# Block sums made in the up projections and kept in DRAM; 49 seven-product pairs instead of 32

## Chip, core and metric

The kernel runs on one core of a Trainium2 chip. The metric is the time of one execution on the device in microseconds (us). Before the change it is 2122.69 us, the median of three runs (2122.64 to 2122.83).

## The reference

A two-layer encoder trunk for 256 tokens of width 2048, all in float32. Each layer has an attention part (differential attention in layer 0, windowed grouped-query attention in layer 1, each beside four heads that look at 256 memory tokens, and one output projection) and a dense MLP. The change lies in the MLP:

```python
x = x + heads @ w_out[i]
h = rms_norm(x, norm_mlp[i])
x = x + jnp.square(jax.nn.relu(h @ w_up[i])) @ w_down[i]     # 2048 -> 8192 -> 2048
```

## The kernel before

**Three products for one.** TensorE multiplies a rounded float32 form. Each operand is split into a rounded part and a remainder by `split`: ScalarE casts (`hi`, L249), VectorE subtracts (`lo`, L250). A product is then hi x hi, hi x lo and lo x hi, added up in PSUM (`three`, L359 to L361). Weights come from DRAM in pieces of 128 x 1024 (512 KB), and every piece is split on arrival.

**Fetching.** `plan` lists all weight pieces in the order of use. `fetch` takes the next one, lets SyncE (SP) load it into a buffer `raw`, and splits it into `hi` and `lo`; there are four buffers of each. `piece` keeps two pieces ahead of the one in use. Other tiles come from three rings of 512 KB buffers: `x2` (8), `h2` (6), `blk` (10).

**The up projections** (L333 and L337) take 16 chunks of 512 columns. ScalarE and VectorE make the squared ReLU of each (L788 to L790) into a hidden tile of 512 KB; six of the sixteen lie in one large buffer (`big`, chunks 4 to 9), the other ten in `blk`. Chunk c holds hidden blocks j = 2c and 2c+1.

**The down projections** run in two halves of 1024 output columns, and in each through j = 0 to 31. A pair j is two weight pieces and one hidden block, which `h2_of` splits into a buffer of `h2`. An ordinary pair multiplies a 2 x 2 of blocks by a 2 x 2 of blocks in eight products, 24 matmuls. For the j in `FAST` (5, 8, ... 26, eight per half) the same result comes from **seven products** (`seven`, 21 matmuls). They need sums of blocks on both sides: of the weights, a and b, made from the two raw pieces in `fetch_sums` (L202, L204, L205) and split in turn into four tiles; of the hidden block, four differences made by `differences` (L370, L372, L373) and split (L249, L250 `h<-t2k`). Both halves make the differences of a block anew. The four extra accumulators (`side`) are folded into the outputs by `shared` after the half's last seven-product pair. The out projections have three such pairs in each layer (`OUT_FAST`).

The two halves use tiles of the same name, but a and b lie in `x2` except in the second half of layer 0, where the next layer's inputs take part of `x2`; there they lie in `blk`, as the hidden tiles come free.

**What sets the order.** The program is written in the order above; small jobs are `Task`s, of which `tick` runs one that is due after every piece, and `flush` all that are left. From this the tile layer's scheduler makes each engine's list of instructions, which is fixed when the program is built: it moves an instruction ahead where its data is ready. An engine works its list in order. A tile waits until the last readers of its buffer are done. SP's list holds all weight loads; POOL's has little: some loads at the start, sums in the memory part, and two masks (L673, L675) on the bias table that comes back into `big` for layer 1 (L671).

Of the kernel before, what the change touches and what calls it, by code (L numbers as in the profile page):

```python
# [14 lines left out]
F32 = mybir.dt.float32  # L15
# [7 lines left out]
P = 128  # L23
# [10 lines left out]
WAIT = 2  # L34
AHEAD = 2
WARM = 16
FAST = (5, 8, 11, 14, 17, 20, 23, 26)
LAM_INIT = 0.8 - 0.6 * math.exp(-0.3 * 0)

G_ATTN, G_MEM, G_MLP = 0, 2 * KT, 4 * KT  # L40
# [8 lines left out]
def trunk(ctx: ExitStack, tc: tile.TileContext, xin, xtok, memin, pos, rel, gcol, rows,  # L49
# [12 lines left out]
    def nm(s):  # L62
        uid[0] += 1
        return f"{s}{uid[0]}"
# [4 lines left out]
    def quad(tag, shape=(P, 2, 2, 256), dt=F32R):  # L69
        return xp.tile(list(shape), dt, tag=tag, name=nm(tag), bufs={"x2": 8, "h2": 6, "blk": 10}[tag])  # L70
# [92 lines left out]
    def flush():  # L163
        while tasks:
            next(t for t in tasks if t.can()).step()
# [9 lines left out]
    def fast_pairs(name, h):  # L175

        if name.startswith("out"):
            return OUT_FAST[h]
        return FAST if name.startswith("down") else ()

    def plan_pairs(name, n):
        plan.extend((name, h, j) for h in range(2) for j in range(2 * n))
# [10 lines left out]
    newest = [None]  # L193
    sums = {}

    def fetch_sums(key, raw, hi, lo):

        first = newest[0]
        out_ = key[0].startswith("out")
        tag = "blk" if out_ or key[:2] == ("down0", 1) else "x2"  # L200
        a, b = quad(tag, (P, 2, 512), F32), quad(tag, (P, 2, 512), F32)
        nc.vector.tensor_tensor(a, first.rearrange("p (a n) -> p a n", a=2),  # L202
                                raw[:, 512:1024].unsqueeze(1).broadcast_to([P, 2, 512]), op=ALU.add)
        nc.vector.tensor_tensor(b[:, 0, :], a[:, 1, :], first[:, 0:512], op=ALU.add)  # L204
        nc.vector.tensor_tensor(b[:, 1, :], b[:, 0, :], raw[:, 0:512], op=ALU.add)  # L205
        split(hi[:, 0:512], lo[:, 0:512], raw[:, 0:512])
        ah, al, bh, bl = [quad("blk" if out_ else "x2", (P, 2, 512)) for _ in range(4)]
        split(ah, al, a)
        split(bh, bl, b)
        sums[key] = (ah, al, bh, bl)  # L210

    def fetch(parts=1, lead=None):

        name, c, j = plan.popleft()
        src = weights[name][c, j]
        raw = wp.tile([P, 1024], F32, tag="raw", name=nm("raw"))
        hi = wp.tile([P, 1024], F32R, tag="hi", name=nm("hi"))
        lo = wp.tile([P, 1024], F32R, tag="lo", name=nm("lo"))
        n = 1024 // parts
        seven = j % 2 == 1 and j // 2 in fast_pairs(name, c)  # L220
        for i in range(parts):
            s = slice(i * n, (i + 1) * n)
            if lead is not None:
                lead(i)
            behind[0] = nc.sync.dma_start(raw[:, s], src[:, s])
            if seven:
                fetch_sums((name, c, j), raw, hi, lo)
            else:
                split(hi[:, s], lo[:, s], raw[:, s])
        newest[0] = raw  # L230
        ready.append(((name, c, j), hi, lo))
# [545 lines left out]

    def mlp(layer, X2, last):
        hT = []
        wide = big([P, 6, 4, S])  # L780
        for c in range(16):
            ps = chunk_out(f"up{layer}", c, 8, lambda k: X2[k], "mm" if c % 2 == 0 else "aux", 2 if c == 0 else 1)
            if c == 0:
                mlp_stats()
            ht = wide[:, c - 4] if 4 <= c < 10 else blk([P, 4, S], F32)
            for o in range(4):
                t = t1k()
                nc.scalar.copy(t, ps[o][:, 256:512])  # L788
                nc.vector.tensor_tensor(t, ps[o][:, 0:256], t, op=ALU.add)
                nc.vector.scalar_tensor_tensor(ht[:, o, :], t, 0.0, t, op0=ALU.max, op1=ALU.mult)  # L790
            hT.append(ht)
        N2 = Halves()

        def hidden(j):
            return hT[j // 2].rearrange("p k s -> p (k s)")[:, (j % 2) * 512:(j % 2) * 512 + 512]

        def h2_of(j):
            t2 = quad("h2", (P, 2, 512))
            split(t2[:, 0, :], t2[:, 1, :], hidden(j))
            return lambda kk, t, part: t2[:, part, kk * S + t * P:kk * S + (t + 1) * P]  # L800


        for half_ in range(2):
            tag = "mm" if half_ == 0 else "aux"
            ps = [[bank(tag) for _ in range(2)] for _ in range(2)]
            chunks = (2 * half_, 2 * half_ + 1)
            fast = fast_pairs(f"down{layer}", half_)
# [12 lines left out]
            held = []  # L820
            for j in range(32):
                if j == fast[0]:
                    side = [bank("aux" if half_ == 0 else "mm") for _ in range(4)]
                two = [piece(f"down{layer}", half_, 2 * j + i) for i in range(2)]
                at = h2_of(j)
                if last and half_ == 1 and j >= 30:
                    held.append((j, two, at))
                    continue
                if j in fast:
                    t2 = quad("h2", (P, 2, 512))  # L830
                    differences(t2, hidden(j))
# [168 lines left out]
```

## Time and profile before

| | |
|---|---|
| median of 3 runs | 2122.69 us |
| profiled execution | 2122.36 us, its span 2120.6 us |
| TensorE clock granted | 1.000 |
| TensorE / VectorE / ScalarE busy | 2110.4 / 1547.2 / 1141.0 us |
| layer 0: up projections | about 425 to 783 us |
| layer 0: down projections | about 783 to 1119 us |
| layer 1: up projections | about 1424 to 1780 us |
| layer 1: down projections | about 1780 us to the end |

The span runs from the first to the last instruction; the execution's own time is 1.76 us longer. PE is TensorE's matmuls, PEld its weight loads (they overlap), DVE is VectorE, ACT ScalarE, POOL GpSimd. A matmul's length is counted to its modelled end, so that neighbours overlap; what one costs is the distance between starts. In timeline rows the first number is the start, the second the length; in brackets is the idle time before it and what ended it. In group rows the numbers are the busy time, the mean length in ns, and the idle time before.

### The profile page before, as it was taken

To read this page: it belongs to the slowest core of one execution; us is meant where nothing else is said; L and a number is where in the kernel's file an instruction comes from. 1 tells how busy PE (TensorE), PEld (TensorE's weight loads), DVE (VectorE), ACT (ScalarE), POOL (GpSimd) and SP (SyncE) were. 2 spreads that over 40 slices of the span, in tenths; PEclk is the share of its full clock that TensorE was granted. 3 is DMA by queue.
4 is the path that set the end of the run, shared out by engine and by line. 5 is a ranking of instruction groups with operands and counts; after the bars stand their busy time and mean duration, and the time that the engine had idled before them with its cause. 6 is when DMAs were issued, how large, how long until landed. Compare 5 with 4: busy or idle time off the path is not lost.

```text
span 2120.6 us, 29406 instructions
## 1 busy us (share of the span) xinstructions
PE 2110.4 (100%) x11002; PEld 1786.8 (84%) x11002; DVE 1547.2 (73%) x2341; ACT 1141.0 (54%) x1732; POOL 34.9 (2%) x61
## 2 busy tenths in 40 slices
PE   9999999999999999999999999999999999999999
PEld 7878878888888888888888888888888888888887
DVE  7667788865565558889986677885655656888896
ACT  6456675554444445656655566564444444665564
POOL 1200020000000000000000000000000000000000
PEclk9999999999999999999999999999999999999999
DMA  8864464566666666565756555455666666566654
GB/s 295 239 210 150 159 192 156 190 181 196 188 188 190 189 189 204 193 200 198 257 200 190 179 168 184 152 190 187 187 190 189 185 195 189 193 216 206 207 190 159
DMA packets 114960, 409.24 MB, mean 193 GB/s; under 512 B 13568, under 2 KB 14336, under 8 KB 114560
## 3 DMA queue, kind: packets, MB, share of 16 engines
q1 hardware_dynamic: 111840, 401.01, 59.2%
q0 software_dynamic: 1536, 4.20, 0.8%
q10 hardware_dynamic: 1440, 2.15, 0.3%
q8 instruction: 86, 1.41, 0.3%
q14 instruction: 58, 0.48, 0.1%
HBM read 401.93 MB, written 5.37 MB: 192 GB/s over the span
## 4 chain that ended last, share of the span: by engine, by line
PE 96%; DMA 1%; DVE 1%; ACT 1%; issue 0%; POOL 0%; DVEq 0%; ACTq 0%; POOLq 0%
PE mm L333 11%; PE aux L333 11%; PE mm L360 7%; PE mm L359 7%; PE mm L361 7%; PE aux L360 7%; PE aux L359 7%; PE aux L361 7%; PE mm L320 6%; PE mm L321 6%; PE mm L322 6%; PE mm L337 6%; PE aux L337 6%; DMA raw<-in_w_a 1%; PE aux L461 1%; PE aux L432 1%
## 5 line engine op out<-in xcount | busy, mean ns | idle before, releaser
L250 DVE TENSOR_TENSOR lo<-raw,hi 128x1024 fp32r<-128x1024 f32 (+1 forms) x744 | 869.6, 1184 | 477.9 <-ACT hi L249 476.7
L249 ACT CAST hi<-raw 128x1024 fp32r<-128x1024 f32 (+1 forms) x744 | 745.9, 1020 | 721.1 <-PE aux L333 193.6
L320 PE MATMUL mm<-hi,x 128*128 128x512 f32 x640 | 256.4, 402 | 1.9 <-ACT hi L249 1.9
L321 PE MATMUL mm<-lo,x 128*128 128x512 f32 x640 | 251.3, 393 | 1.6 <-DVE lo L250 1.6
L322 PE MATMUL mm<-hi,x 128*128 128x512 f32 x640 | 250.9, 392 | 0.0
L333 PE MATMUL mm<-x,hi 128*128 128x512 f32 x1024 | 246.9, 391 | 0.0
L333 PE MATMUL aux<-x,hi 128*128 128x512 f32 x1024 | 246.9, 391 | 0.0
L333 PEld LDWEIGHTS mm<-x,hi 128*128 128x128 f32 x1024 | 188.2, 188 | 36.4
L333 PEld LDWEIGHTS aux<-x,hi 128*128 128x128 f32 x1024 | 188.2, 188 | 36.4
L359 PE MATMUL mm<-hi,h 128*128 128x512 f32 x518 | 202.0, 390 | 0.0
L360 PE MATMUL mm<-lo,h 128*128 128x512 f32 x518 | 201.6, 389 | 0.0
L361 PE MATMUL mm<-hi,h 128*128 128x512 f32 x518 | 201.6, 389 | 0.0
L359 PE MATMUL aux<-hi,h 128*128 128x512 f32 x502 | 195.5, 390 | 0.0
L360 PE MATMUL aux<-lo,h 128*128 128x512 f32 x502 | 195.4, 389 | 0.0
L361 PE MATMUL aux<-hi,h 128*128 128x512 f32 x502 | 195.4, 389 | 0.0
L320 PEld LDWEIGHTS mm<-hi,x 128*128 128x128 f32 x640 | 120.2, 188 | 26.3 <-ACT hi L249 3.1
L321 PEld LDWEIGHTS mm<-lo,x 128*128 128x128 f32 x640 | 120.6, 188 | 25.0 <-DVE lo L250 3.1
L322 PEld LDWEIGHTS mm<-hi,x 128*128 128x128 f32 x640 | 120.2, 188 | 25.3
L337 PEld LDWEIGHTS aux<-x,lo 128*128 128x128 f32 x1024 | 131.3, 191 | 5.0
L337 PEld LDWEIGHTS mm<-x,lo 128*128 128x128 f32 x1024 | 131.1, 191 | 4.8
L337 PE MATMUL mm<-x,lo 128*128 128x256 f32 x1024 | 133.0, 283 | 0.0
L337 PE MATMUL aux<-x,lo 128*128 128x256 f32 x1024 | 132.8, 283 | 0.0
(259 smaller groups left out, 2514.5 us busy)
## 6 DMA issues: line engine op xcount, KB each, us to landing
raw<-in_w_up SPq DMA_DIRECT2D x256, 512.0 KB, 4.2
raw<-in_w_down SPq DMA_DIRECT2D x256, 512.0 KB, 4.3
raw<-in_w_a SPq DMA_DIRECT2D x72, 512.0 KB, 3.7
raw<-in_w_out SPq DMA_DIRECT2D x64, 512.0 KB, 3.7
raw<-in_w_b SPq DMA_DIRECT2D x48, 512.0 KB, 3.7
raw<-in_w_mem SPq DMA_DIRECT2D x32, 512.0 KB, 3.8
raw<-in_w_a SPq DMA_DIRECT2D x16, 256.0 KB, 5.5
blk<-bkt POOLq DMA_DIRECT2D x32, 128.0 KB, 8.7
```

What stands on the lines that cost most here:

```text
L249: nc.scalar.copy(hi, src)
L250: nc.vector.tensor_tensor(lo, src, as32(hi), op=ALU.subtract)
L320: nc.tensor.matmul(ps[t], lhsT=xh, rhs=hi[:, ws], start=(k == 0), stop=False)
L321: nc.tensor.matmul(ps[t], lhsT=xh, rhs=lo[:, ws], start=False, stop=False)
L322: nc.tensor.matmul(ps[t], lhsT=xl, rhs=hi[:, ws], start=False, stop=(k == KT - 1))
L333: nc.tensor.matmul(ps[o], lhsT=hi[:, cols(k % 2, o)], rhs=x2.rearrange("p a s -> p (a s)"), start=(k == 0), stop=(k == 2 * nj - 1))
L337: nc.tensor.matmul(ps[o][:, 256:512], lhsT=lo[:, cols(k % 2, o)], rhs=x2[:, 0, :], start=False, stop=False)
L359: nc.tensor.matmul(acc_, lhsT=x(0), rhs=w2[0][:, ws], start=first_, stop=False)
L360: nc.tensor.matmul(acc_, lhsT=x(0), rhs=w2[1][:, ws], start=False, stop=False)
L361: nc.tensor.matmul(acc_, lhsT=x(1), rhs=w2[0][:, ws], start=False, stop=last_)
L432: nc.tensor.transpose(out=pt[:, h * P:(h + 1) * P], in_=qn[t][:, h * P:(h + 1) * P], identity=ident)
L461: nc.tensor.transpose(out=pt[:, kt * S + qt * P:kt * S + (qt + 1) * P], in_=p_of(qt)[:, kt * P:(kt + 1) * P], identity=ident)
```

## The change

Three things. First, `FAST` now holds every odd j from 3 to 27, thirteen per half; in the second half of layer 0 the list is `LATE`, every odd j from 9 to 27, ten. That makes 13 + 10 + 13 + 13 = 49 seven-product pairs in the down projections, where there were 32. Second, the differences of a hidden block are made once, in a Task two ticks after its chunk of the up projections (`keep`), split, and stored by POOL in DRAM (`kept`); a seven-product pair lets POOL load them into its `h2` tile. Third, the raw pieces of a seven-product pair no longer lie in the four `raw` buffers but in the ring that holds their sums (`spare`: `blk` for the out projections and for the second half of layer 0's down projections, else `x2`); the same goes for the out projections' three pairs. The hidden chunks in `big` are now 6 to 11.

```diff
-FAST = (5, 8, 11, 14, 17, 20, 23, 26)
+FAST = tuple(range(3, 28, 2))
+LATE = tuple(range(9, 28, 2))
...
-        return FAST if name.startswith("down") else ()
+        if name.startswith("down"):
+            return LATE if (name, h) == ("down0", 1) else FAST
+        return ()
...
+    def spare(name, c):
+        return "blk" if name.startswith("out") or (name, c) == ("down0", 1) else "x2"
+
     def fetch_sums(key, raw, hi, lo):
...
-        out_ = key[0].startswith("out")
-        tag = "blk" if out_ or key[:2] == ("down0", 1) else "x2"
+        tag = spare(*key[:2])
...
-        raw = wp.tile([P, 1024], F32, tag="raw", name=nm("raw"))
+        seven_ = j // 2 in fast_pairs(name, c)
+        raw = quad(spare(name, c), (P, 1024), F32) if seven_ else wp.tile([P, 1024], F32, tag="raw", name=nm("raw"))
...
-        seven = j % 2 == 1 and j // 2 in fast_pairs(name, c)
...
-            if seven:
+            if seven_ and j % 2 == 1:
                 fetch_sums((name, c, j), raw, hi, lo)
...
+        def keep(j):
+
+            t2 = quad("h2", (P, 2, 512))
+            differences(t2, hidden(j))
+            kept[j] = dp.tile([P, 2, 512], F32R, name=nm("kept"))
+            nc.gpsimd.dma_start(kept[j], t2)
+
...
-            ht = wide[:, c - 4] if 4 <= c < 10 else blk([P, 4, S], F32)
+            ht = wide[:, c - 6] if 6 <= c < 12 else blk([P, 4, S], F32)
...
+            for j in (2 * c, 2 * c + 1):
+                if any(j in fast_pairs(f"down{layer}", h) for h in range(2)):
+                    Task([lambda j=j: keep(j)], wait=2)
...
+        flush()
...
                 if j in fast:
                     t2 = quad("h2", (P, 2, 512))
-                    differences(t2, hidden(j))
+                    nc.gpsimd.dma_start(t2, kept[j])
                     seven(ps, side, j == fast[0], j == fast[-1], two, sums.pop((f"down{layer}", half_, 2 * j + 1)), at, t2)
```

In the changed kernel a line past the helpers stands some lines lower (L202 is L207 there, L250 is L255, L225 is L230).

**VectorE, first half of layer 0's down projections.** Before, the end of a round of three pairs: the remainders of an ordinary pair (`lo_8254`, `lo_8260`), two hidden splits, then the sums and remainders of a seven-product pair (its raw pieces are 8291 and 8297).

```order
L250 TENSOR_TENSOR lo_8254<-raw_8252,hi_8253 128x1024
L250 TENSOR_TENSOR lo_8260<-raw_8258,hi_8259 128x1024
L250 TENSOR_TENSOR h_8398<-big_4668,h_8398 128x512
L250 TENSOR_TENSOR h_8450<-big_4668,h_8450 128x512
L202 TENSOR_TENSOR x_8301<-raw_8291,raw_8297 128x1024
L204 TENSOR_TENSOR x_8302<-x_8301,raw_8291 128x512
L205 TENSOR_TENSOR x_8302<-x_8302,raw_8297 128x512
L250 TENSOR_TENSOR x_8309<-x_8301,x_8308 128x1024
L250 TENSOR_TENSOR x_8311<-x_8302,x_8310 128x1024
L250 TENSOR_TENSOR lo_8293<-raw_8291,hi_8292 128x1024
L250 TENSOR_TENSOR lo_8299<-raw_8297,hi_8298 128x512
L250 TENSOR_TENSOR h_8489<-big_4668,h_8489 128x512
```

In the changed kernel one whole round, of two pairs: the seven-product pair 11 (raw pieces x_8422 and x_8428), then the ordinary pair 12.

```order
L255 TENSOR_TENSOR lo_8424<-x_8422,hi_8423 128x1024
L207 TENSOR_TENSOR x_8432<-x_8422,x_8428 128x1024
L255 TENSOR_TENSOR lo_8430<-x_8428,hi_8429 128x512
L209 TENSOR_TENSOR x_8433<-x_8432,x_8422 128x512
L255 TENSOR_TENSOR h_8576<-big_4668,h_8576 128x512
L210 TENSOR_TENSOR x_8433<-x_8433,x_8428 128x512
L255 TENSOR_TENSOR x_8440<-x_8432,x_8439 128x1024
L255 TENSOR_TENSOR x_8442<-x_8433,x_8441 128x1024
L255 TENSOR_TENSOR lo_8476<-raw_8474,hi_8475 128x1024
L255 TENSOR_TENSOR lo_8482<-raw_8480,hi_8481 128x1024
L255 TENSOR_TENSOR h_8627<-big_4668,h_8627 128x512
```

The remainder of the first raw piece now stands ahead of the sums, which stand between other instructions; the differences and their split (`h<-t2k`) are gone from the round, which has eleven instructions.

**SP at the same place.** Before, all raw pieces in the order of their use:

```order
L225 DMA raw_8252<-in_w_down 128x1024
L225 DMA raw_8258<-in_w_down 128x1024
L225 DMA raw_8291<-in_w_down 128x1024
L225 DMA raw_8297<-in_w_down 128x1024
L225 DMA raw_8343<-in_w_down 128x1024
L225 DMA raw_8349<-in_w_down 128x1024
```

In the changed kernel, where x_ are the raw pieces of seven-product pairs:

```order
L230 DMA raw_8474<-in_w_down 128x1024
L230 DMA raw_8480<-in_w_down 128x1024
L230 DMA x_8422<-in_w_down 128x1024
L230 DMA x_8428<-in_w_down 128x1024
L230 DMA raw_8564<-in_w_down 128x1024
L230 DMA raw_8570<-in_w_down 128x1024
```

The ordinary pair 12 (8474, 8480) is now asked for ahead of pair 11 (8422, 8428).

**POOL, end of layer 0's down projections.** Before, the masks follow the sums of layer 0's memory part:

```order
L262 TENSOR_TENSOR acc<-acc,t1k_3453 128x256
L262 TENSOR_TENSOR acc<-acc,t1k_3456 128x256
L262 TENSOR_TENSOR acc<-acc,t1k_3459 128x256
L262 TENSOR_TENSOR acc<-acc,t1k_3462 128x256
L673 AFFINE_SELECT big_10736<-big_10736 128x12x128
L675 AFFINE_SELECT big_10736<-big_10736 128x12x128
```

In the changed kernel they follow the loads of the stored differences for pairs 23, 25 and 27, and stand ahead of layer 1's stores:

```order
L848 DMA h_10471<-kept_7216 128x1024
L848 DMA h_10561<-kept_7422 128x1024
L848 DMA h_10651<-kept_7628 128x1024
L678 AFFINE_SELECT big_10857<-big_10857 128x12x128
L680 AFFINE_SELECT big_10857<-big_10857 128x12x128
L795 DMA kept_14232<-h_14225 128x1024
L795 DMA kept_14438<-h_14431 128x1024
```

POOL thus issues the differences' loads and stores, 49 and 26, in the order of their use.

More of the change, by code (lines that the diff above doesn't have):

```diff
@@ L206, in fetch_sums @@
         split(hi[:, 0:512], lo[:, 0:512], raw[:, 0:512])
-        ah, al, bh, bl = [quad("blk" if out_ else "x2", (P, 2, 512)) for _ in range(4)]
+        ah, al, bh, bl = [quad("blk" if key[0].startswith("out") else "x2", (P, 2, 512)) for _ in range(4)]
         split(ah, al, a)
@@ L779, in mlp, with hidden @@
         hT = []
+        kept = {}
         wide = big([P, 6, 4, S])
+        def hidden(j):
+            return hT[j // 2].rearrange("p k s -> p (k s)")[:, (j % 2) * 512:(j % 2) * 512 + 512]
+        def keep(j):
[3 more added lines that the diff above has]
+            nc.gpsimd.dma_start(kept[j], t2)
         for c in range(16):
@@ L791, in mlp @@
             hT.append(ht)
+            for j in (2 * c, 2 * c + 1):
+                if any(j in fast_pairs(f"down{layer}", h) for h in range(2)):
+                    Task([lambda j=j: keep(j)], wait=2)
         N2 = Halves()
-        def hidden(j):
-            return hT[j // 2].rearrange("p k s -> p (k s)")[:, (j % 2) * 512:(j % 2) * 512 + 512]
         def h2_of(j):
```

## The prediction

> **What bounds the kernel now.** I read the page's first lines and its chain first, then what TensorE waited for, then the busy time by stage.
>
> ```profile
> span 2120.6 us, 29406 instructions
> PE 2110.4 (100%) x11002; PEld 1786.8 (84%) x11002; DVE 1547.2 (73%) x2341; ACT 1141.0 (54%) x1732; POOL 34.9 (2%) x61
> PE 96%; DMA 1%; DVE 1%; ACT 1%; issue 0%; POOL 0%; DVEq 0%; ACTq 0%; POOLq 0%
> PE mm L320 <- ACT hi L249: 1.9, 2, 1.2
> PE mm L321 <- DVE lo L250: 1.6, 1, 1.6
> 425.00:783.00 358.00, 358.00 (x2066) 316.56 (x2064) 208.95 (x286) 160.05 (x211) 0.00 (x0) 1.00 0.62 189
> 783.00:960.00 177.00, 177.00 (x786) 146.67 (x785) 151.44 (x184) 105.40 (x137) 0.00 (x0) 1.00 0.59 197
> ```
>
> TensorE is idle for 10 us of 2120.6, and the chain is its own work. The last two rows are layer 0's up projections and the first part of its down projections; the columns are length, busy time of PE, PEld, DVE, ACT and POOL, clock, DMA share, GB/s. TensorE never stops in either, at full clock. So a matmul that goes is worth its spacing, as long as what feeds it keeps up. VectorE is the feeder to watch: 151 of 177 us in the down projections, 209 of 358 in the up projections.
>
> **What the change takes from TensorE.** The timeline shows the starts of two neighbouring seven-product pairs (three pairs apart, as FAST was):
>
> ```profile
> 840.80 0.39 PE L359 MATMUL aux<-hi,h 128*128 128x512 f32 x1
> 856.44 0.39 PE L359 MATMUL aux<-hi,h 128*128 128x512 f32 x1
> ```
>
> Between them lie 21 + 24 + 24 = 69 matmuls in 15.64 us: 0.2267 us each (0.39 is one's own length; they overlap). An ordinary pair is 24 x 0.2267 = 5.44 us, a seven-product pair 21 x 0.2267 = 4.76 us, so each conversion is worth 0.68 us. The pairs go from 4 x 8 = 32 to 13 + 10 + 13 + 13 = 49: **17 x 0.68 = 11.56 us**. The built program has 51 TensorE rows fewer, which is 17 x 3.
>
> **What it asks of VectorE.** A seven-product pair now comes every second pair, so one of each kind must be fed in 5.44 + 4.76 = 10.20 us. The first rows below are an ordinary pair's work, the others a seven-product pair's where nothing held VectorE up:
>
> ```profile
> 1029.81 0.69 DVE L250 TENSOR_TENSOR h<-t2k,h 128x512 fp32r<-128x512 f32 x1
> 1030.41 2.35 DVE L250 TENSOR_TENSOR lo<-raw,hi 128x1024 fp32r<-128x1024 f32 x2
> 1032.68 1.28 DVE L250 TENSOR_TENSOR h<-big,h 128x512 fp32r<-128x512 f32 x2
> 1052.22 1.21 DVE L202 TENSOR_TENSOR blk<-raw,raw 128x1024 f32<-128x1024 f32 x1
> 1053.36 1.21 DVE L250 TENSOR_TENSOR lo<-raw,hi 128x1024 fp32r<-128x1024 f32 x1
> ...
> 1058.04 1.21 DVE L250 TENSOR_TENSOR x<-blk,x 128x1024 fp32r<-128x1024 f32 x1
> 1059.17 3.48 DVE L250 TENSOR_TENSOR lo<-raw,hi 128x1024 fp32r<-128x1024 f32 x3
> ```
>
> Starts count, since an instruction's end overlaps the next. Two weight remainders take 1032.68 - 1030.41 = 2.27 us and one hidden split 1030.41 - 1029.81 = 0.60: 2.87 us for an ordinary pair. The seven-product pair's eight instructions (three sums, two remainders of the raw pieces, two of the sums, one hidden split) take 1059.17 - 1052.22 = 6.95 us. Together **9.82 us of 10.20**: VectorE keeps up with 0.38 us to spare, where it now has some 2 us per three pairs.
>
> This only closes because the block sums leave the stage. Today they cost it, per seven-product pair:
>
> ```profile
> 791.36 0.42 DVE L370 TENSOR_TENSOR t2k<-blk 128x256 f32<-128x256 f32 x1
> 791.82 0.29 DVE L372 TENSOR_TENSOR t2k<-blk,t2k 128x128 f32<-128x128 f32 x1
> 792.15 0.29 DVE L373 TENSOR_TENSOR t2k<-blk,t2k 128x128 f32<-128x128 f32 x1
> ```
>
> With the split of the result (0.69 above) that is 1.7 us; left in, the two pairs would need 11.5 us. In the up projections it is made 13 times a layer, 22 us more on a VectorE that is busy 209 of 358 us: nothing, while that cover lasts.
>
> The order within the two pairs matters as well. Let t = 0 be the start of the ordinary pair, which is the end of the last but one seven-product pair and so frees hi and lo. A cast takes 1.05 us (row below); VectorE then runs its 6.95 us from 1.1 to 8.05. The last result of these is wanted at 5.44 + 16 x 0.2267 = 9.07. The next ordinary pair's remainders are ready at 9.2 and 10.3, wanted at 10.43 and 11.1. VectorE is free at 10.92, and the next cast is done at 11.25. Nothing is late, by 0.8 us at the least. ScalarE has 1.05 + 0.61 + 2 x 1.06 + 0.62 = 4.4 us of casts for the one kind and 2 x 1.05 + 0.62 = 2.7 for the other, 7.1 of 10.2 (groups of three such pairs):
>
> ```profile
> L249 ACT CAST hi<-raw 128x1024 fp32r<-128x1024 f32 x16 | 16.5, 1049 | 6.8 <-issue 5.4 <-DMA raw<-in_w_down 1.4
> L249 ACT CAST h<-big 128x512 fp32r<-128x512 f32 x5 | 3.0, 622 | 0.1
> L249 ACT CAST hi<-raw 128x512 fp32r<-128x512 f32 x3 | 1.8, 614 | 0.0
> L249 ACT CAST x<-x 128x1024 fp32r<-128x1024 f32 x6 | 6.3, 1055 | 10.4 <-DVE x L202 9.2 <-DVE x L205 1.2
> ```
>
> **What it asks of the DMA engines.** Two pairs now load four raw pieces and one stored sum, 5 x 0.524 MB = 2.62 MB in 10.20 us: 257 GB/s. The windows row has 197 GB/s at a share of 0.59, so about 0.77; and a short stretch in which the bias table came back carried more with TensorE never idle:
>
> ```profile
> 1025.00:1050.00 25.00, 25.00 (x113) 20.68 (x111) 21.86 (x24) 15.53 (x19) 3.58 (x2) 1.00 0.89 336
> L225 SPq DMA_DIRECT2D raw<-in_w_down x68: 327/328/442, 783.0 to 959.4; - x68
> DMA to landing us min/median/max: 3.4/4.2/5.3
> blk<-bkt POOLq DMA_DIRECT2D x32, 128.0 KB, 8.7
> ```
>
> A seven-product pair's first raw piece now takes the buffer of the pair's before, free after the first half of its sum b. From there: landing, cast 1.05, remainder 1.14, sum a 1.14, the other remainder 0.6, that half of b 0.6, some 0.15 of semaphores: landing + 4.7 us must stay under 10.20. At 4.2 it is 8.9, at the longest seen, 5.3, it is 10.0. The ordinary pairs keep four raw buffers to themselves. A stored sum's load waits for the seven-product pair two before, and is wanted 5.44 + 4.76 + 5.44 = 15.6 us later; POOL's loads land in 8.7. Cost: nothing, and no longer nothing beyond a landing of 5.5 us.
>
> **What POOL's issues cost VectorE.** These are three answers of the timeline: POOL issuing, VectorE at that time, and POOL's mask work with VectorE behind it:
>
> ```profile
> 49.32 4.51 POOL L650 DMA_DIRECT2D blk<-bkt  x9 [25.34 <-DMA bkt<-t1k]
> 50.02 1.23 DVE L250 TENSOR_TENSOR lo<-raw,hi 128x1024 fp32r<-128x1024 f32 x1 [1.69 <-ACT hi L249]
> 51.67 1.23 DVE L250 TENSOR_TENSOR lo<-raw,hi 128x1024 fp32r<-128x1024 f32 x1 [0.43 <-ACT hi L249]
> 1045.31 1.62 POOL L673 TENSOR_SCALAR_AFFINE_SELECT big<-big 128x1536 f32<-128x1536 f32 x1 [740.05 <-DMA big<-bsv]
> 1045.44 2.03 DVE L250 TENSOR_TENSOR h<-t2k,h 128x512 fp32r<-128x512 f32 x1
> 1047.45 2.57 DVE L250 TENSOR_TENSOR h<-blk,h 128x512 fp32r<-128x512 f32 x2
> ```
>
> Nine issues in a row did not lengthen a remainder (1.23 us as elsewhere), so I take nothing for the 75 new ones. The Trainium skill ("SBUF — State Buffer", section "Who interferes with whom") gives the other side: a VectorE instruction with two SBUF inputs, as these all are, blocks and is blocked by a GpSimd instruction that reads SBUF, while making descriptors only writes (which the page calls inferred). By that the sum stays; if issuing also read, it would be the third rival below. The mask work did lengthen VectorE's, by 1.35 + 1.29 = 2.64 us. It now falls among seven-product pairs with little to spare: the next ordinary pair's first remainder, ready at 9.2, comes at 11.84 against 10.43, so TensorE loses **1.4 us**, once (bounds: 0 if it falls after the last such pair, 2.64 with no slack left).
>
> **The rest.** Each half enters and leaves the denser stretch once; before and after lie ordinary pairs with 2.6 us of VectorE time free each, and the first pair's sums are made while up projections run. Bounds 0 and 1 us a half; I take **0.6 us** in all. In the out projections three pairs' raw pieces move to blk: no instruction is added, 0 to 1 us either way, taken as 0.
>
> **The sum.** The profiled run took 2122.36 us (span 2120.6). 2122.36 - 11.56 + 1.4 + 0.6 = 2112.8; the median of the runs is 0.33 above the profiled run, so **2113.1 us**. Its own range is 2110.5 to 2116.
>
> **The rivals.**
> 1. *Stalls at the edges* (0.18). Bounds above all at their upper end: 2.64 + 4 x 1 + 1 = 7.6 instead of 2.0: 2118.7 at most, about 2117.
> 2. *VectorE becomes the bound* (0.13), the case on the other side. The even pairs recur 12 + 9 + 12 + 12 = 45 times. Each microsecond beyond 10.20 is then paid 45 times; the 9.6 us of gain are used up at 10.41 us for two pairs, only 0.59 over my 9.82. Now VectorE often stands before a sum, for raw pieces:
>
> ```profile
> 817.40 1.23 DVE L202 TENSOR_TENSOR x<-raw,raw 128x1024 f32<-128x1024 f32 x1 [0.80 <-DMA raw<-in_w_down]
> 848.44 1.23 DVE L202 TENSOR_TENSOR x<-raw,raw 128x1024 f32<-128x1024 f32 x1 [0.55 <-DMA raw<-in_w_down]
> ```
>
> If such a gap, 0.8 us, remained: 10.62, a loss of 0.42 x 45 = 18.9, hence 2132. For: four engines have to meet within 1 us. Against: those gaps came while VectorE had time to spare, and the sums have earlier raw pieces and no shared buffers now.
> 3. *POOL's issues hold VectorE off* (0.04). 0.49 us an issue (its length on POOL for 32 rows; 4.51 us for nine): 10.31, 45 x 0.11 = 5 us back: 2118. With 128 rows four times that: 11.78, and 2184.
> 4. *Raw pieces land late* (0.07). At 5.8 us the loop is 10.5: 0.3 x 36 (the halves on x2) = 10.8 back, 2124, no change; at 6.5 slower by 25 us. For: a third more traffic. Against: the stored sums and the pieces start at different times of the two pairs.
> 5. *The change does less than it says* (0.02): excluded on TensorE by the 51 rows.
>
> Forecast 0.56. What a measurement can tell from no change is 0.2%, 4.2 us. Faster by more: 0.56 + 0.18 + half of the third = 0.76, of which I leave 0.01 for what I don't see; within it 0.10; slower 0.15. The range takes in rival 1 and no more of the rest than the fifth allowed: 2110.5 to 2122.
>
> **What would show it.** In the changed profile: TensorE's spacing from one seven-product pair to the next is 10.20 us in all four halves and its waits on VectorE in the down projections stay under 3 us; VectorE there is over 95% busy with remainders still 1.21 to 1.23 us; raw pieces land in under 5.3 us; the mask work costs one gap near 1040. A spacing of 10.4 or more, with VectorE idle before a sum, would prove rival 2; the same with long remainders, rival 3; idle VectorE on a late raw piece, rival 4.

## The result

The changed kernel takes **2109.81 us** (median of four runs, 2109.66 to 2110.09); the kernel before took 2122.76 beside it (2122.64 to 2123.86). The ratio is 0.9938, with a 95% interval of 0.9921 to 0.9955. Measured again on another occasion (run *repeat* below) it took 2111.16 against 2121.96, ratio 0.9948 (0.9935 to 0.9960). Forecast were 2113.1 us and a range from 2110.5: the sign and the main term were right, the first time lies 3.3 us below the forecast and 0.7 us below the range, the second inside the range.

### The profile page after: what moved, and what is told of

The parts are those of the page before. It is cut to its first block, busy times and chain, and to the rows that moved or that the text cites. A ratio compares the mean times of both kernels' runs of the same rounds, so it can differ in the third digit from the quotient of the medians.

```text
span 2107.9 us, 29757 instructions
## 1 busy us (share of the span) xinstructions
PE 2098.7 (100%) x10951; PEld 1777.3 (84%) x10951; DVE 1603.4 (76%) x2402; ACT 1164.8 (55%) x1760; POOL 77.2 (4%) x136
## 4 chain that ended last, share of the span: by engine, by line
PE 96%; DMA 1%; DVE 1%; ACT 1%; issue 0%; SPq 0%; POOL 0%; ACTq 0%; DVEq 0%; POOLq 0%
PE mm L338 11%; PE aux L338 11%; PE aux L365 7%; PE aux L366 7%; PE aux L364 7%; PE mm L365 7%; PE mm L366 7%; PE mm L364 7%; PE mm L325 6%; PE mm L326 6%; PE mm L327 6%; PE mm L342 6%; PE aux L342 6%; DMA raw<-in_w_a 1%; PE aux L466 1%; PE aux L437 1%
## 5 line engine op out<-in xcount | busy, mean ns | idle before, releaser
L255 DVE TENSOR_TENSOR lo<-raw,hi 128x1024 fp32r<-128x1024 f32 (+1 forms) x634 | 761.8, 1213 | 398.6 <-ACT hi L254 395.4
L254 ACT CAST hi<-raw 128x1024 fp32r<-128x1024 f32 (+1 forms) x634 | 650.2, 1040 | 674.9 <-PE aux L338 188.4
L364 PE MATMUL aux<-hi,h 128*128 128x512 f32 x470 | 183.0, 390 | 0.0
L365 PE MATMUL aux<-lo,h 128*128 128x512 f32 x470 | 183.0, 389 | 0.0
L366 PE MATMUL aux<-hi,h 128*128 128x512 f32 x470 | 182.9, 389 | 0.0
L364 PE MATMUL mm<-hi,h 128*128 128x512 f32 x465 | 181.4, 390 | 0.0
L365 PE MATMUL mm<-lo,h 128*128 128x512 f32 x465 | 181.0, 389 | 0.0
L366 PE MATMUL mm<-hi,h 128*128 128x512 f32 x465 | 181.0, 390 | 0.0
```

Of the source, the lines that this page charges most:

```text
L254: nc.scalar.copy(hi, src)
L255: nc.vector.tensor_tensor(lo, src, as32(hi), op=ALU.subtract)
L364: nc.tensor.matmul(acc_, lhsT=x(0), rhs=w2[0][:, ws], start=first_, stop=False)
L365: nc.tensor.matmul(acc_, lhsT=x(0), rhs=w2[1][:, ws], start=False, stop=False)
L366: nc.tensor.matmul(acc_, lhsT=x(1), rhs=w2[0][:, ws], start=False, stop=last_)
```

## The profile after

The first lines of the changed kernel's page and all its TensorE waits of a microsecond or more:

```profile
span 2107.9 us, 29757 instructions
PE 2098.7 (100%) x10951; PEld 1777.3 (84%) x10951; DVE 1603.4 (76%) x2402; ACT 1164.8 (55%) x1760; POOL 77.2 (4%) x136
PE mm L326 <- DVE lo L255: 1.9, 1, 1.9
PE aux L466 <- DVE t2k L505: 1.2, 1, 1.2
PE aux L117 <- DVE tab L634: 1.1, 1, 1.1
```

None of these waits lies in the down projections; all were there before, nearly as long. In the down projections (a window in the middle of layer 0's first half; columns as in the prediction) and at the starts of three seven-product pairs there:

```profile
825.00:907.00 82.00, 82.00 (x363) 67.91 (x362) 81.01 (x92) 54.92 (x65) 4.31 (x8) 1.00 0.80 258
858.51 0.39 PE L364 MATMUL aux<-hi,h 128*128 128x512 f32 x1
868.71 0.39 PE L364 MATMUL aux<-hi,h 128*128 128x512 f32 x1
878.91 0.39 PE L364 MATMUL aux<-hi,h 128*128 128x512 f32 x1
```

TensorE never stops, two pairs take 10.20 us to the hundredth, VectorE is busy 81.01 of 82 us, and the traffic is 258 GB/s at a share of 0.80 (predicted: 10.20, over 95%, 257 at 0.77).

Where the 12.7 us between the two profiles come from is read off the starts of the same matmuls in both. First the end of the first projection, which no part of the change touches, then the first and the last matmul of the down projections; the kernel before, then the changed one:

```profile
61.26 0.50 PE L661 MATMUL aux<-tab,blk 128*128 128x48 bf16 x13
782.32 0.39 PE L359 MATMUL mm<-hi,h 128*128 128x512 f32 x1
2116.45 0.39 PE L361 MATMUL aux<-hi,h 128*128 128x512 f32 x1
```

```profile
59.47 0.50 PE L666 MATMUL aux<-tab,blk 128*128 128x48 bf16 x13
780.99 0.39 PE L364 MATMUL mm<-hi,h 128*128 128x512 f32 x1
2103.76 0.39 PE L366 MATMUL aux<-hi,h 128*128 128x512 f32 x1
```

In the same way for every stage (first to last matmul, us). Between the halves of layer 0 the transposes for the next stage come in after the second half's first pair; "first half" here runs to these transposes and "second half" starts behind them:

| | before | after | difference |
|---|---|---|---|
| start to the end of the first projection | 61.26 | 59.47 | -1.79 |
| layer 0, down, first half (5 pairs more) | 173.85 | 170.45 | -3.40 |
| layer 0, down, second half (2 more) | 157.63 | 156.27 | -1.36 |
| layer 1, down, both halves (10 more) | 337.29 | 330.48 | -6.81 |
| all else | | | +0.67 |

The three down rows are 5, 2 and 10 times 0.68 us to within 0.01, together 11.57. Of the 0.67 the two out projections have 0.47 (70.25 us each before, 70.54 and 70.43 after); the up projections are equal. So three things differ from the sum on record: none of its 2.0 us of losses is there, 1.8 us were gained in a place where both kernels do the same, and 0.7 us were lost elsewhere.

## The experiments

Unless a ratio is given, lengths of the down stages are compared, since they hold nothing of the start. They are layer 0's halves and layer 1; before 173.85, 157.63, 337.29; after 170.45, 156.27, 330.48.

**The two other parts without the list.** The lists go back to one pair in three:

```diff
-FAST = tuple(range(3, 28, 2))
-LATE = tuple(range(9, 28, 2))
+FAST = (5, 8, 11, 14, 17, 20, 23, 26)
+LATE = (11, 14, 17, 20, 23, 26)
```

> Stored sums and own raw buffers stay, but the seven-product pairs go back to one in three: 8 + 6 + 8 + 8 = 30. Theory 1 (only TensorE's matmuls count, 0.68 us a pair, the other two parts neither cost nor bring anything): 19 pairs more to pay than in the changed kernel, 2109.8 + 12.9 = 2122.7 if the start stays as early as there (first projection over at 59.2 us), 2124.4 if the early start belongs to the list of pairs or to chance (over at 61.0). Theory 2 (the stored sums or the buffers bring time by themselves, 2 us or more): 2120.5 or less with the late start.

Measured: 2124.81 us beside 2123.19 for the kernel before, ratio 1.0011 (1.0002 to 1.0020); down stages 173.85, 158.99, 337.31. Two pairs fewer than before cost 1.36 us in the half they were taken from, and the other stages equal the old ones to 0.02 us. Without the longer list, the stored sums and the own buffers bring nothing and cost nothing in the down projections. Theory 2 falls.

**The differences back in the down projections.** The Tasks that run `keep` go; a seven-product pair makes its differences again:

```diff
-                    nc.gpsimd.dma_start(t2, kept[j])
+                    differences(t2, hidden(j))
```

> 49 pairs and own raw buffers stay; the differences of a hidden block are made and split in the down projections again, once per half, and nothing is stored in DRAM. Theory 1 (VectorE has 10.20 us for two pairs and now needs 9.8): with 1.7 us more it needs 11.5, and each of the 45 rounds costs 1.3 us: 2109.8 + 58 = 2168, less what is made ahead of its round. Rival (VectorE's margin, or work done ahead, takes it up): under 2115. For the start: if the DRAM tiles make it early, the first projection ends at 61.0 us here as in the kernel before; if it has nothing to do with them, it may end at 59.2.

Measured: 2134.60 us, ratio 1.0059 (1.0042 to 1.0075); down stages 177.30, 159.08, 344.21, so 23 us more than with stored sums, not 58. TensorE in the last rounds of the first half:

```profile
895.34 0.50 PE L364 MATMUL aux<-x,h 128*128 128x512 f32 x1 [0.72 <-ACT x L254]
907.19 0.50 PE L364 MATMUL aux<-x,h 128*128 128x512 f32 x1 [0.70 <-ACT x L254]
919.05 0.51 PE L364 MATMUL aux<-x,h 128*128 128x512 f32 x1 [0.71 <-ACT x L254]
```

These rounds take 11.85 us, a little over the reckoned 11.5, but only the last ones cost anything. The lead, here the time from the start of sum a to the first use of a sum, tells why. In the changed kernel, sum a of the first pair is begun while up projections still run, and that of a middle pair 7.6 us before its first use (VectorE's row, then TensorE's, for both):

```profile
773.16 1.23 DVE L207 TENSOR_TENSOR x<-x,x 128x1024 f32<-128x1024 f32 x1 [0.79 <-DMA x<-in_w_down]
799.35 0.39 PE L364 MATMUL aux<-x,h 128*128 128x512 f32 x1
...
863.18 1.22 DVE L207 TENSOR_TENSOR x<-x,x 128x1024 f32<-128x1024 f32 x1
866.72 2.48 DVE L255 TENSOR_TENSOR x<-x,x 128x1024 fp32r<-128x1024 f32 x2
870.75 0.39 PE L364 MATMUL aux<-x,h 128*128 128x512 f32 x1
```

The first lead is 26 us. Without stored sums it melts, from 25 us (first pair) over 7 (fifth) to 3.1 us (last four, 925.60 to 928.74 for the last), and only then does TensorE wait. A stretch before the waits, then ScalarE and VectorE in a round with a wait:

```profile
860.00:889.00 29.00, 29.00 (x127) 23.30 (x126) 29.00 (x41) 18.55 (x24) 0.00 (x0) 1.00 0.62 206
898.62 0.62 ACT L254 CAST h<-blk 128x512 fp32r<-128x512 f32 x1 [3.33 <-PE aux L366]
899.27 0.69 DVE L255 TENSOR_TENSOR h<-blk,h 128x512 fp32r<-128x512 f32 x1 [1.05 <-ACT h L254]
```

While the lead melts, VectorE is busy without a gap (29.00 of 29 us) and TensorE loses nothing. In the last rounds VectorE is no longer full: it stands 1.05 us before a hidden split, because the cast for it waits 3.33 us in ScalarE's list for a matmul to free its buffer. Followed through the trace, the round is a closed loop: matmuls to 898.6, this cast, VectorE from 899.27 to 906.06, the cast of sum b, and the matmul that waited, at 907.19. So VectorE's own work alone does not set the 11.85 us. Theory 1 comes near the rate, has the wrong number of rounds, and does not have the bound of the last rounds. The 23 us are the cost of taking the stored sums away; how they divide between VectorE's work and this wait stays open.

**The raw pieces back in the common buffers.**

```diff
-        raw = quad(spare(name, c), (P, 1024), F32) if seven_ else wp.tile([P, 1024], F32, tag="raw", name=nm("raw"))
+        raw = wp.tile([P, 1024], F32, tag="raw", name=nm("raw"))
```

> The raw pieces of seven-product pairs come out of the four common raw buffers again; the rest is as in the changed kernel. Theory 1 (with one of each kind in turn, a piece takes the buffer of the piece four before, which is the same piece of the last seven-product pair in either ring, so the own buffers bring nothing): 2109.8 +- 1. Rival (the common buffers make pieces late, which is why they were parted): at least 0.3 us in each of 45 rounds, 2123 or more, with VectorE waiting for raw pieces ahead of the sums.

Measured: 2152.24 us, ratio 1.0138 (1.0123 to 1.0153); down stages 178.35, 170.95, 350.79, so 43 us more. My theory fell and the rival holds: the third part of the change, worth nothing without the longer list, is worth 43 us together with the others. VectorE's groups between 800 and 930 us, first with common buffers, then in the changed kernel:

```profile
L207 DVE TENSOR_TENSOR x<-raw,raw 128x1024 f32<-128x1024 f32 x12 | 14.7, 1224 | 12.7 <-DMA raw<-in_w_down 12.7
```

```profile
L207 DVE TENSOR_TENSOR x<-x,x 128x1024 f32<-128x1024 f32 x11 | 13.4, 1219 | 0.0
```

VectorE stood 12.7 us before sum a, waiting for raw pieces. One turn of that loop, with common buffers:

```profile
869.79 0.69 DVE L210 TENSOR_TENSOR x<-x,raw 128x512 f32<-128x512 f32 x1
870.54 0.33 SPq L230 DMA_DIRECT2D raw<-in_w_down  x1
875.56 1.23 DVE L207 TENSOR_TENSOR x<-raw,raw 128x1024 f32<-128x1024 f32 x1 [1.61 <-DMA raw<-in_w_down]
876.71 3.49 DVE L255 TENSOR_TENSOR lo<-raw,hi 128x1024 fp32r<-128x1024 f32 x3
880.11 0.69 DVE L209 TENSOR_TENSOR x<-x,raw 128x512 f32<-128x512 f32 x1
881.32 0.69 DVE L210 TENSOR_TENSOR x<-x,raw 128x512 f32<-128x512 f32 x1
```

The last reader of the old piece starts at 869.79, the load at 870.54, the sum 5.0 us later, and in this round three remainders of 128x1024 stand in VectorE's list between the sum and the last reader (881.32): a turn of 11.5 us, where 10.20 are to be had. In every other round one stands there and the turn is 9.9; in the changed kernel none does (863.18 to 866.12). Four turns from 847.82 to 891.14 average 10.83 us; 0.63 over in twelve rounds is 7.6 us, about the 7.9 that this half lost. It is the prediction's own raw loop, held open longer. This is read from the trace of the first half; the two runs below ask what in the buffers does it.

**SP starts the loads in the order of use.** The buffers are those of the changed kernel:

> The changed kernel with all its buffers, but SP must start the loads of the down projections in the order of use. In the changed kernel it starts an ordinary pair's pieces ahead of the seven-product pair's that come before it. Theory 1 (what the own raw buffers bring is this early load: an ordinary pair's pieces are there when VectorE would otherwise wait for a sum's): the loss of the kernel with common buffers comes back, some 20 us in each layer, 2140 to 2152. Theory 2 (the number of buffers matters, not the order of loads): within 3 us of the changed kernel.

```diff
-            behind[0] = nc.sync.dma_start(raw[:, s], src[:, s])
+            if name.startswith("down") and j > 0:
+                with tc.issue_after(behind[0].ins):
+                    behind[0] = nc.sync.dma_start(raw[:, s], src[:, s])
+            else:
+                behind[0] = nc.sync.dma_start(raw[:, s], src[:, s])
```

Measured: 2110.80 us, ratio 0.9947 (0.9932 to 0.9962); down stages 170.63, 156.31, 331.19, 0.9 us more in all. The early start of the ordinary pieces is not what the buffers bring. Theory 2.

**Two ordinary buffers in place of four.** The same on the other tile with the tag `raw`:

```diff
-        raw = quad(spare(name, c), (P, 1024), F32) if seven_ else wp.tile([P, 1024], F32, tag="raw", name=nm("raw"))
+        raw = quad(spare(name, c), (P, 1024), F32) if seven_ else wp.tile([P, 1024], F32, tag="raw", name=nm("raw"), bufs=2)
```

> The changed kernel with two common raw buffers in place of four, so that an ordinary pair's piece again takes the buffer of the ordinary pair before, as it does where all share four. The up projections get longer by it and are not compared; the down stages are. Theory 1 (what the own buffers bring is that the ordinary pairs have four to themselves): the down stages get about as long as with common buffers, 178.4 us in the first half of layer 0 and 350.8 us in layer 1 where the changed kernel takes 170.5 and 330.5. Theory 2 (it is the seven-product pairs that need buffers of their own): 171 and 331.

One run, 2299.31 us, most of it lost elsewhere, as expected. Down stages 170.41, 163.12, 345.75: 22 of the 43 us, none of them in layer 0's first half. Neither theory fits. That the ordinary pairs' spare buffers carry part of the gain is likely from the other two stages, but one run that changes so much else does not show it; how the gain is divided stays open.

**The list alone.** The kernel before with the new lists and nothing else:

```diff
-FAST = (5, 8, 11, 14, 17, 20, 23, 26)
+FAST = tuple(range(3, 28, 2))
+LATE = tuple(range(9, 28, 2))
...
-        return FAST if name.startswith("down") else ()
+        return (LATE if (name, h) == ("down0", 1) else FAST) if name.startswith("down") else ()
```

> The kernel before with the longer lists alone, 49 pairs: differences made in each half, raw pieces in the common buffers. Theory 1 (both other parts are needed, and their losses, 23 and 43 us, add up as VectorE is the loser in both): 2111 + 66 = 2177. Theory 2 (the waits for raw pieces leave VectorE the time that the differences need, so the larger loss stands alone): 2154. Rival (the list by itself brings the gain): under 2122.

Measured: 2143.48 us, ratio 1.0102 (1.0084 to 1.0121); down stages 178.74, 162.82, 347.67, so 32 us more than the changed kernel. The list by itself makes the kernel slower; but the losses neither add up (66) nor is the larger one the floor (43). Here VectorE does not wait before sum a at all:

```profile
L203 DVE TENSOR_TENSOR x<-raw,raw 128x1024 f32<-128x1024 f32 x12 | 14.6, 1215 | 0.0
```

With the differences in its list it is busy 129.46 of these 130 us, so the raw loop finds no gap to open. TensorE's longest waits in this kernel end with ScalarE's cast of a hidden block (14.1 us in nine waits, all in the down projections); what delays it, and why 9 us more are lost than without the stored sums alone, stays open.

**Mask work in the middle.** What the prediction charged with 1.4 us, put where it was charged:

```diff
+                    if layer == 0 and half_ == 0 and j in (9, 13, 17, 21):
+                        for i in range(6):
+                            m = t2k([P, 512])
+                            nc.gpsimd.affine_select(out=m, in_=as32(t2)[:, i % 2, :], pattern=[[0, 4], [-1, P]],
+                                                    compare_op=ALU.is_ge, fill=NEG, base=0, channel_multiplier=1)
```

> Mask work on GpSimd is added in the middle of layer 0's first down half, four times six selects of 128x512 whose output nobody reads, each lot once in two rounds. Theory 1 (the prediction's price is right and only its place was wrong: it fell behind the last seven-product pair): each lot costs VectorE about 2.6 us, of which 1.2 or so is margin the first time and 0.8 is won back in two rounds, so 1.4 to 1.8 us a lot and 2115 to 2117. Rival (TensorE has enough ahead, or VectorE is not held up, and mask work costs nothing wherever it stands): 2109.8 +- 0.5.

Measured: 2118.19 us, ratio 0.9974 (0.9964 to 0.9983); that half takes 176.61 us, 6.2 more, the other stages are unchanged (156.27, 330.49). VectorE under one lot, GpSimd's row first:

```profile
864.81 7.92 POOL L852 TENSOR_SCALAR_AFFINE_SELECT t2k<-h 128x512 f32<-128x512 f32 x6 [8.62 <-DMA h<-kept]
...
865.90 1.12 DVE L255 TENSOR_TENSOR h<-big,h 128x512 fp32r<-128x512 f32 x1
867.12 1.47 DVE L255 TENSOR_TENSOR lo<-x,hi 128x1024 fp32r<-128x1024 f32 x1
868.52 1.65 DVE L207 TENSOR_TENSOR x<-x,x 128x1024 f32<-128x1024 f32 x1
```

Instructions of 0.69 us take 1.12, one of 1.22 takes 1.65, until the lot ends. TensorE lost nothing at the first lot (the lead took it) and 1.9, 2.1 and 2.1 us at the others. Theory 1: the price is of the right size where VectorE's lead is used up, and nothing where it is not.

**One VectorE instruction more.** In `fetch_sums`, behind `split(bh, bl, b)`:

```diff
+        if key[0].startswith("down"):
+            m = t2k([P, 512])
+            nc.vector.tensor_tensor(m, as32(bl)[:, 0, 0:512], b[:, 0, 0:512], op=ALU.add)
```

> One more VectorE instruction of 128x512 (0.60 us) in every seven-product pair of the down projections, behind the sums; nobody reads what it writes. Theory 1 (the prediction's reckoning: two pairs need 9.82 + 0.60 = 10.42 of 10.20, and each of the 45 rounds pays 0.22): 10 us. Theory 2 (VectorE enters each half some 5 us ahead, as the kernel without stored sums showed, where rounds of 11.4 us cost TensorE nothing for the first seven; 12 x 0.22 = 2.7 us a half is less than that): 0 to 2 us.

Measured: 2116.99 us, ratio 0.9977 (0.9968 to 0.9987); down stages 171.19, 156.68, 334.64, so 5.3 us more, between the theories (10, and 0 to 2). VectorE's new instruction recurs every 10.55 us:

```profile
2000.59 0.68 DVE L217 TENSOR_TENSOR t2k<-x,x 128x512 f32<-128x512 f32 x1
2011.15 0.68 DVE L217 TENSOR_TENSOR t2k<-x,x 128x512 f32<-128x512 f32 x1
2021.70 0.69 DVE L217 TENSOR_TENSOR t2k<-x,x 128x512 f32<-128x512 f32 x1
```

Less the 0.60 that were added, VectorE's own round is 9.95 us (predicted 9.82). At 0.35 over TensorE's, 45 rounds would cost 16 us; 5.3 were paid. The lead carries the rest.

**The same kernel again**, with no edit, beside the kernel before and others:

> The changed kernel as it is, beside the others and the kernel before on one chip. The five profiles so far have the same instructions at the start, but their first projection ends between 58.97 and 61.04 us. If the start is chance, before and changed kernel differ by 17 x 0.68 - 0.5 = 11.1 us in the median over many runs here; if the early start belongs to the changed kernel, by 12.7 or more.

Measured: 2111.16 us (2109.73 to 2113.06) beside 2121.96 (2120.87 to 2124.41), 10.8 us apart. Its down stages are 170.45, 156.27, 330.47 again, but its first projection ends at 60.22 us and not at 59.47:

```profile
60.22 0.95 PE L666 MATMUL aux<-tab,blk 128*128 128x48 bf16 x31
```

Over the thirteen profiles of these kernels but *raw_two* this point lies between 59.20 and 62.73 us, with stored sums and without, behind the same instructions on every engine. So the early start does not belong to the change; it was luck that it favoured the changed kernel by 1.8 us in the first pair of profiles. Whether it differs from one execution to the next is not shown: the four first runs of the changed kernel agreed to 0.4 us, while nineteen of the kernel before on another occasion lay between 2120.29 and 2125.70.

**More pairs.** First 29 in every half, and 1 in the last:

```diff
-FAST = tuple(range(3, 28, 2))
-LATE = tuple(range(9, 28, 2))
+FAST = tuple(range(3, 30, 2))
+LATE = tuple(range(9, 30, 2))
+LAST = tuple(range(1, 30, 2))
...
-            return LATE if (name, h) == ("down0", 1) else FAST
+            return {("down0", 1): LATE, ("down1", 1): LAST}.get((name, h), FAST)
```

> More seven-product pairs: 29 is added in every half and 1 in the last, which makes 54. Theory (each is worth 0.68 us, VectorE keeps up): 5 x 0.68 = 3.4 us less than the changed kernel. Rival (with j = 29 the four extra accumulators are folded in and freed only after the half's last pair, so the next half waits for its banks, and VectorE, with the first sums early, has no ordinary pairs to catch up in): as much lost at the ends of the halves, no gain or a loss.

Measured: 2124.09 us, ratio 1.0008 (0.9999 to 1.0017): no gain over the kernel before is left. Down stages 173.24, 155.59, 341.27. The second half of layer 0 does gain its 0.68. The first half loses 3.5 us at its start, where TensorE waits for VectorE's remainders. The last half has rounds of 11.3 us, with ScalarE waiting for TensorE (ScalarE's waits there, then in the changed kernel):

```profile
ACT h L255 <- PE mm L367: 32.8, 10, 3.4
```

```profile
ACT h L254 <- PE mm L366: 3.3, 6, 0.7
```

In each of ten rounds the cast of a hidden block stands first in ScalarE's list and waits 3.3 us for its `h2` buffer, with the casts of the raw pieces behind it. The same wait stands in *no_keep*'s last rounds. The order was written when the program was built, and no engine lacks the time; this is read from the trace, and no run moves the cast. Neither clause of the rival named it.

Then 29 alone, with its differences made in place, as the only ones:

```diff
-FAST = tuple(range(3, 28, 2))
-LATE = tuple(range(9, 28, 2))
+FAST = tuple(range(3, 30, 2))
+LATE = tuple(range(9, 30, 2))
...
-                if any(j in fast_pairs(f"down{layer}", h) for h in range(2)):
+                if j < 28 and any(j in fast_pairs(f"down{layer}", h) for h in range(2)):
...
-                    nc.gpsimd.dma_start(t2, kept[j])
+                    if j in kept:
+                        nc.gpsimd.dma_start(t2, kept[j])
+                    else:
+                        differences(t2, hidden(j))
```

> j = 29 is added in every half (53 pairs), as in the kernel with 54, but its differences are made in the down projections and not stored; j = 1 in the last half is left out. Theory (of what the 54 lost, 3.4 and 1.6 us were lost at the start of the first halves, where the thirteenth or later stored sum held VectorE up, and 12 in the half that begins at j = 1; j = 29 itself cost nothing in the second half of layer 0): 4 x 0.68 = 2.7 us less than the changed kernel, which took 2111.16 in the last comparison. Rival (VectorE's 1.7 us for the differences, or the fold-in before the next half, cost it at the end of each half): 0 to 4 us more.

Measured: 2109.34 us, ratio 0.9940 (0.9927 to 0.9954), against 0.9948 (0.9935 to 0.9960) for the changed kernel in *repeat*; the totals don't tell them apart. The down stages do: 169.77, 155.59, 329.85, so 2.0 us less of the 2.7 expected. By its down stages it is the shortest of these kernels.

**The out projections' pieces back in the common buffers.** The own buffers are kept for the down projections alone:

```diff
-        raw = quad(spare(name, c), (P, 1024), F32) if seven_ else wp.tile([P, 1024], F32, tag="raw", name=nm("raw"))
+        raw = quad(spare(name, c), (P, 1024), F32) if seven_ and name.startswith("down") else wp.tile([P, 1024], F32, tag="raw", name=nm("raw"))
```

> The changed kernel with the out projections' three pairs a layer in the common raw buffers, as before. If their move to the other ring makes the out projections longer in the trace (70.54 and 70.43 us where they were 70.25 in both layers), they are 70.25 here again, and 0.5 us is gained; otherwise they stay as they are.

One run. The out projections take 70.25 and 70.25 us again, the down stages are those of the changed kernel (170.45, 156.27, 330.47). First expectation. The price of the move is small and not steady: the two stages together are 0.08 to 0.52 us longer than 140.50 in the nine profiles that have it (0.47 and 0.32 in two of the same kernel), and exactly 140.50 in the four without, *raw_two* left out.

## Why the prediction was off

Step by step, as the prediction put them:

- **TensorE, 17 x 0.68 = 11.56.** Right: 11.57, and in each of the three stages by itself.
- **VectorE, 9.82 of 10.20.** Right in kind, 0.13 too small: 9.95 measured. That the differences must leave the stage and that the raw pieces must not share buffers is shown by *no_keep* and *raw_shared*.
- **"Nothing is late, by 0.8 us at the least."** Nothing was late, but the 0.8 us are the step that failed, and with it the two losses that were built on it. The reckoning starts its clock at the end of a seven-product pair, which is said to free hi and lo. But `seven` reads the pair's own hi and lo in the first three of its seven products only; the other four read the sums. So they come free nine matmuls into the pair, 12 x 0.2267 = 2.7 us before its end. The pair that starts at 878.91 ends at 883.67, and the next cast into its hi starts when a matmul frees it (first row). The other rows are an ordinary pair's two remainders and their first uses:

```profile
881.19 1.05 ACT L254 CAST hi<-x 128x1024 fp32r<-128x1024 f32 x1 [0.19 <-PE mm L366]
869.37 2.36 DVE L255 TENSOR_TENSOR lo<-raw,hi 128x1024 fp32r<-128x1024 f32 x2 [0.17 <-ACT hi L254]
873.70 0.39 PE L365 MATMUL mm<-lo,h 128*128 128x512 f32 x1
874.38 0.39 PE L365 MATMUL mm<-lo,h 128*128 128x512 f32 x1
```

  VectorE is done with the seven-product pair's work at 869.20, 5.9 us after the ordinary pair's start at 863.27, where 8.05 was reckoned. The remainders are done at 870.59 and 871.73 and wanted at 873.70 and 874.38: 3.1 and 2.6 us ahead, where 1.2 and 0.8 were reckoned. At the start of the half the lead is larger still (26 us from sum a to its use). The **mask work's 1.4 us** came to 0, and the **edges' 0.6 us** came to 0. That a lead takes up a delay is shown by the first lot of *mask_mid*; that the early release of hi and lo makes this one is read from the program and the trace, and no run changes it. For the mask work the place was wrong as well: it fell beside the last pair's sums, and not among pairs:

```profile
1075.01 2.97 POOL L678 TENSOR_SCALAR_AFFINE_SELECT big<-big 128x1536 f32<-128x1536 f32 x1 [0.65 <-DMA big<-bsv]
1077.77 1.30 DVE L207 TENSOR_TENSOR blk<-blk,blk 128x1024 f32<-128x1024 f32 x1 [1.19 <-DMA blk<-in_w_down]
1079.20 3.48 DVE L255 TENSOR_TENSOR lo<-raw,hi 128x1024 fp32r<-128x1024 f32 x2
```

  VectorE lost 1.2 us to a late piece and at least 1.1 to the masks there (3.48 for two remainders, 2.36 elsewhere), and TensorE nothing. The prediction's lower bound, 0 if the masks fall after the last such pair, comes nearest to this case, and it was not taken.
- **DMA.** Right in the middle: in the halves on `x2` the raw pieces land in 4.2 to 4.9 us in the median. But single pieces there take up to 7.5 us in layer 0 and 8.1 in layer 1, and in the second half of layer 0 those in `blk` take 5.6 in the median and 11.9 at most, beside the bias table. The sign "raw pieces land in under 5.3 us" is missed, and the limit of 5.5, beyond which a loss was foretold, was passed without one: the profile shows no wait of TensorE in the down projections. The limit counted every round by itself and left out the lead.
- **POOL's issues, 0.** Right: 75 more of them, 0.54 us each, and remainders still take 1.22 us. The Trainium skill ("SBUF — State Buffer", section "Who interferes with whom") says that a VectorE instruction with two SBUF inputs contends with a GpSimd instruction that reads SBUF and not with one that only writes it, and it counts making descriptors, as inferred, among the writes. The trace agrees on both: the issues left such instructions at their length, and the selects of *mask_mid*, which read SBUF, lengthened them from 0.69 to 1.12 us.
- **The out projections, 0.** Mis-sized: +0.47 us in the profiled run, 0.08 to 0.52 in others, inside the bounds.
- **The range.** With no loss at all the steps give 2111.1, so its low end of 2110.5 left 0.6 us for everything unforeseen. The start alone moves by over 3 us between profiles, and it was chance that it fell early in the first comparison: in *repeat* the time lies inside the range, and the two kernels are 10.8 us apart where 9.6 were forecast. That the three runs before agreed within 0.2 us was taken for the spread of a comparison; the median of the kernel before was 2122.76, 2123.19, 2121.96 and 2121.66 in four of them. Term by term for the profiled run: 2122.36 - 11.57 - 1.79 + 0.67 = 2109.67.
- **Rival 2's price**, "each microsecond beyond 10.20 is paid 45 times": wrong by the same lead. In *dve_512* 0.35 us over cost 5.3 us and not 16, and in *no_keep* the reckoned 1.3 us over cost 23 and not 58.

## What to carry to other kernels

A feeder with less work than the engine it feeds builds up a lead; before a lost microsecond on it is charged, read from the trace how far ahead of its use the last product is ready, and at what rate the lead melts. Parts of a change may bring nothing without the others and still each be needed: leaving out the stored sums cost 23 us here and leaving out the own buffers 43, the two together without the list brought nothing, and the list by itself cost 22 (2143.48 against 2121.66). When hi and lo come free is read from which products use them, not from the end of the pair. And a range needs room for what differs between two occasions with the same instructions, which a few runs in a row need not show.

## What the runs showed that was not expected

- The first 60 us differ by over 3 us between profiles of the same instructions. Between 10 and 20 us the kernel before moved 319 GB/s with TensorE busy 8.94 us, the changed one 359 GB/s and 9.59 us:

```profile
10.00:20.00 10.00, 8.94 (x37) 6.53 (x36) 6.97 (x16) 5.66 (x14) 0.00 (x0) 1.00 0.94 319
```

```profile
10.00:20.00 10.00, 9.59 (x40) 7.38 (x41) 8.86 (x20) 7.65 (x18) 0.00 (x0) 1.00 1.02 359
```

  What makes the loads faster or slower was not tried.
- In three of the four lots of *mask_mid*, six selects of 128x512 took 7.9 to 8.6 us on GpSimd beside a busy VectorE, and held VectorE up by about 0.4 us each. The first lot's row is 18.4 us long, and for its first 9 us VectorE's instructions kept their lengths; what held the selects there is not shown.
